# Where the last tile's norm stands at the end of two output products

## Chip, core and metric

The kernel runs on one core of a Trainium2 chip. The metric is the device time of one execution in microseconds (us); the median of several runs is given. TensorE (PE) does the matrix products, ScalarE (ACT) activations and casts, VectorE (DVE) sums of two tiles, GpSimd (POOL) here little beside the roots of the norms, SyncE (SP) issues most DMAs.

## The reference

Two layers over 1024 tokens of 1024 features. The first mixes by attention, the second by a recurrent block; both end with a dense SwiGLU block. Each sub-layer is normed before and behind:

```python
for layer in range(DEPTH):
    h = rmsnorm(x, norm_mix_pre[layer])
    m = attention_mixer(h, ...) if layer % 2 == 0 else recurrent_mixer(h, ...)
    x = x + rmsnorm(m, norm_mix_post[layer])
    h = rmsnorm(x, norm_ffn_pre[layer])
    x = x + rmsnorm(swiglu(h, ...), norm_ffn_post[layer])
```

Both mixers end with a product by an output matrix, `m = y @ w_out`. What matters here is the stretch from that product through the two norms to the first gate and up products of SwiGLU.

## The kernel before

**Precision and tiles.** Most products take each operand as a sum of two rounded parts (hi and lo) and make three passes: hi by hi, hi by lo, lo by hi. Tokens go in eight tiles of 128.

**The output product** (`out_product`, called once in each layer) runs over tiles 0 to 2, then 3 to 5, then 6 and 7, each time over eight blocks of the inner size. The last four blocks of tiles 6 and 7 are done in plain float32 (L662, matmuls at L585), so that their weights need no split; they sit in buffers of the tag "w".

**The norm of a tile** (`norm`, which calls `post_norm_of`, and `pre_norm`) has these steps:

- first squares on ACT (L178 through `rstd`), of the product in PSUM, summed along the row;
- the root of the mean on POOL (L182, L183);
- the gain of the post norm on DVE (L250), which reads the same PSUM tile as the squares and is run behind them;
- the residual on DVE (L256): rows times root plus x; it is stored by SP (L258);
- second squares on ACT (L178 again) of the new x, and their root on POOL (L182, L183);
- the scaling by that root on ACT (L212), called `scaled`;
- the turn: eight transposes on PE (L222) into two PSUM tiles;
- the take (`HiddenS.take`): ACT copies both out (L85), DVE forms four sums of blocks in the one buffer of the tag "tf", ACT casts to the hi parts (L96) and DVE subtracts for the lo parts (L89).

**The gate's operands.** SwiGLU's products are made by Strassen's scheme in seven products of blocks. `first` calls `gate_load`, which scales the gate's weights by the gain of the norm (L700) and forms their sums and differences on DVE (L719 to L726), with a cast (L712) and a subtraction (L713) for each of seven operands. Then it sets up the seven products over the first 256 columns, which come from tiles 0 to 3. `strassen` is a generator: the caller draws products from it, so that PE has work between the turns of the last tiles: one product, tile 6's turn, four products, tile 7's turn, two products. Next come the same seven products over the other 256 columns, which need tiles 4 to 7, and then the up product (`gate_up`), whose weights are scaled behind the last cast of tile 7's take.

**What sets the order.** A planner puts every engine's instructions in a fixed order: among those that it takes to be ready it picks by rank. `behind` adds edges to it: each instruction traced inside the block comes after the named ones that run on the same engine. It makes no wait between engines. Each engine then works through its list in that order. `last_m` holds the first squares (ACT) and the gain (DVE) of a tile; `first` returns `last`, the last cast (ACT) and the last subtraction (DVE) of the gate's operands.

Of the kernel before, what the change touches and what calls it, by code (L numbers as in the profile page):

```python
# [12 lines left out]
ALU = mybir.AluOpType  # L13
# [14 lines left out]
def rows(t, x):  # L28

    if not isinstance(t, tuple):  # L30
        return [(slice(0, P), x[t * P:(t + 1) * P, :])]
    r, a = t
    o = [2 * a * P + k * P + 64 * r for k in range(2)]
    return [(slice(64 * k, 64 * k + 64), x[o[k]:o[k] + 64, :]) for k in range(2)]
# [65 lines left out]
class Trunk:  # L100
# [134 lines left out]
    def post_norm_of(self, ms, mg, x_src, x_dst, t, gpost, sink, pool, x=None):  # L235

        nc = self.nc
        if x is None:  # L240
            x = pool.tile([P, D], F32, tag="nx", bufs=2, name=self.uid("x"))
        for d, s in rows(t, x_src):
            self.load(x[d, :], s)
        junk = pool.tile([P, D // len(ms)], BF16, tag="junk", bufs=1, name=self.uid("junk"))

        squares_first = mg is ms[0][1] or len(ms) == 1
        if squares_first:
            rs = self.rstd(pool, [m for _, m in ms], junk)
        for c, m in ms:
            scaled = nc.vector.tensor_tensor(mg[:, c], m, gpost[:, c], op=ALU.mult).ins  # L250
        if not squares_first:
            rs = self.rstd(pool, [m for _, m in ms], junk)
        self.last_m = [self.squared, scaled]

        def rest(later=False):
            nc.vector.scalar_tensor_tensor(x, mg, rs, x, op0=ALU.mult, op1=ALU.add)  # L256
            for k, (d, s) in enumerate(rows(t, x_dst)):
                (nc.scalar if k and sink is None else nc.sync).dma_start(s, x[d, :])  # L258
            if sink is not None:
                return self.pre_norm(pool, x, mg, None, sink, t, self.psum_t, later)  # L260

        return rest
# [299 lines left out]
    def out_product(self, ap, pp, first, aT, w, x_src, x_dst, gpost_v, sink, kts):  # L562

        nc = self.nc
# [16 lines left out]
        def matmuls(ps, passes, first, last):  # L581

            for n in range(2):
                for i, (x, y) in enumerate(passes):
                    self.matmul = nc.tensor.matmul(ps[:, n * 512:(n + 1) * 512], x, y[:, n, :], start=first and i == 0,  # L585
                                     stop=last and i == len(passes) - 1).ins

        def norm(t, ps):
            mg = ap.tile([P, D], F32, tag="mg", bufs=3, name=self.uid("mg"))

            x = self.apool.tile([P, 1152], F32, tag="first", name=self.uid("x"))[:, :D] if t in (2, 5) else None
            return self.post_norm_of([(slice(0, D), ps)], mg, x_src, x_dst, t, gpost, sink, ap, x)
# [6 lines left out]
        for t0 in (0, 3):  # L599
# [30 lines left out]
            last_m = self.last_m  # L630
# [27 lines left out]
        for t in range(2):  # L658
            for i in range(4):

                with self.behind([self.matmul] + ([self.turned[3 + i]] if t == 0 and i < 3 else [])):
                    matmuls(pst[t], [(acts[i][:, t * P:(t + 1) * P], rows[i])], False, i == 3)  # L662
            if t == 0:
                rest = norm(6, pst[0])
                last_m = self.last_m
                turn6 = rest(True)
                scaled = self.scaled


        last, products, hold = first(last_m, psum)  # L670
        with self.behind([scaled, *last]):
            rest = norm(7, pst[1])
        last_m = self.last_m
        turn7 = rest(True)
# [577 lines left out]
```

## Time and profile before

| | |
|---|---|
| median of 3 runs | 2198.3 us (2197.07 to 2202.79) |
| the profiled execution, its own time | 2198.43 us |
| its span | 2196.6 us |
| PE busy | 2161.5 us (98%) |
| DVE busy | 1540.9 us (70%) |
| ACT busy | 1171.1 us (53%) |
| POOL busy | 217.7 us (10%) |
| granted TensorE clock, mean | 0.997 |

Busy time says how long an engine had an instruction in hand. The span is the time from the first to the last instruction; the time of an execution holds 1.8 us more. A timeline lists instructions of an engine by their start, and in brackets how long it had stood idle and whose result ended that. The granted clock is the share of full speed that PE was given. PE is nearly always busy, so what can be won without less work lies in the few places where it waits or runs at a lower clock.

### The profile page before, as it was taken

The numbers are of one execution on the slowest core, as the hardware profiler recorded it, in microseconds if no ns is written. First come the engines' busy times: TensorE is split into PE (matmuls) and PEld (weight loads), VectorE is DVE, ScalarE is ACT, GpSimd is POOL, SyncE is SP. The second block draws the span as 40 slices with busy tenths as digits, with TensorE's granted clock in tenths as the row PEclk, the third lists the DMA queues.
The fourth block names the chain that finished last, engine by engine and source line by source line (L and its number), as shares of the span: only waits on it lengthen the run. The fifth ranks groups of instructions, "written<-read, shape, count | busy, mean of one in ns | idle before, by whom it ended". The sixth has DMA issues, their size and how long they took to land.

```text
span 2196.6 us, 30590 instructions
## 1 busy us (share of the span) xinstructions
PE 2161.5 (98%) x11140; PEld 1803.2 (82%) x11140; DVE 1540.9 (70%) x2526; ACT 1171.1 (53%) x2174; POOL 217.7 (10%) x450
## 2 busy tenths in 40 slices
PE   9999999999999999999999999999999999999998
PEld 8888889878788888888887777888788888888886
DVE  5877865656878777776767677437787777758675
ACT  6655555556755444443446676528754444424443
POOL 2111113121100000000001333102000000000011
PEclk9999999999999999999999999999999999999999
DMA  7101011126323333336468411356233333328565
GB/s 273 34 30 49 27 37 49 54 84 221 137 91 111 117 98 115 94 123 230 144 183 253 130 58 39 100 192 221 86 120 106 101 112 99 115 87 287 172 182 155
DMA packets 168279, 270.21 MB, mean 123 GB/s; under 512 B 13889, under 2 KB 94785, under 8 KB 168129
## 3 DMA queue, kind: packets, MB, share of 16 engines
q1 hardware_dynamic: 167488, 266.18, 37.8%
q10 hardware_dynamic: 640, 2.10, 0.3%
q8 instruction: 87, 1.43, 0.3%
q14 instruction: 64, 0.52, 0.1%
HBM read 202.69 MB, written 65.54 MB: 122 GB/s over the span
## 4 chain that ended last, share of the span: by engine, by line
PE 87%; DVE 5%; DMA 3%; ACT 3%; issue 2%; POOL 0%; SPq 0%; POOLq 0%; ACTq 0%; DVEq 0%
PE ps L742 12%; PE ps L744 12%; PE ps L743 12%; PE ps L585 8%; PE ps L827 5%; PE ps L829 5%; PE ps L828 5%; PE tr L427 3%; PE pso L356 3%; PE psq L166 2%; PE psq L167 2%; PE psq L168 2%; PE ps L166 2%; PE ps L167 2%; PE ps L168 2%
## 5 line engine op out<-in xcount | busy, mean ns | idle before, releaser
L742 PE MATMUL ps<-hS,q 128*128 128x512 f32 (+1 forms) x1288 | 490.2, 381 | 0.7 <-ACT hS L96 0.4
L743 PE MATMUL ps<-hS,q 128*128 128x512 f32 (+1 forms) x1288 | 489.6, 380 | 0.9 <-DVE hS L89 0.9
L744 PE MATMUL ps<-hS,q 128*128 128x512 f32 (+1 forms) x1288 | 489.0, 380 | 0.0
L713 DVE TENSOR_TENSOR q<-raw,q 128x512 fp32r<-128x512 f32 x308 | 204.5, 685 | 181.6 <-ACT q L712 181.0
L743 PEld LDWEIGHTS ps<-hS,q 128*128 128x128 f32 x1288 | 242.7, 188 | 47.7 <-DVE hS L89 1.3
L742 PEld LDWEIGHTS ps<-hS,q 128*128 128x128 f32 x1288 | 242.3, 188 | 47.3 <-ACT hS L96 0.8
L744 PEld LDWEIGHTS ps<-hS,q 128*128 128x128 f32 x1288 | 242.7, 188 | 45.9
L712 ACT CAST q<-raw 128x512 fp32r<-128x512 f32 x308 | 177.7, 616 | 162.5 <-DVE raw L721 129.4
L828 PE MATMUL ps<-o,o 128*128 128x512 f32 x616 | 240.0, 390 | 0.5 <-DVE o L823 0.5
L829 PE MATMUL ps<-o,o 128*128 128x512 f32 x616 | 238.0, 390 | 0.5 <-DVE o L957 0.5
L700 ACT ACTIVATE raw<-raw,gcol 128x256 f32<-128x256 f32 x352 | 150.3, 498 | 143.3 <-DMA raw<-in_ffn_w_up_dram 71.6
L827 PE MATMUL ps<-o,o 128*128 128x512 f32 x616 | 221.4, 391 | 3.3 <-ACT o L956 3.0
L822 ACT CAST o<-raw 128x512 fp32r<-128x512 f32 x184 | 110.8, 621 | 160.3 <-PE ps L829 59.1
L182 POOL TENSOR_SCALAR rs<-ss 128x1 f32<-128x1 f32 x52 | 24.6, 473 | 1423.6 <-ACT junk L178 1356.9
L823 DVE TENSOR_TENSOR o<-raw,o 128x512 fp32r<-128x512 f32 x184 | 123.1, 686 | 56.1 <-ACT o L822 55.3
L827 PEld LDWEIGHTS ps<-o,o 128*128 128x128 f32 x616 | 115.5, 188 | 30.2 <-ACT o L956 4.8
L828 PEld LDWEIGHTS ps<-o,o 128*128 128x128 f32 x616 | 115.6, 188 | 25.3 <-DVE o L823 1.5
L829 PEld LDWEIGHTS ps<-o,o 128*128 128x128 f32 x616 | 115.6, 188 | 25.1 <-DVE o L957 1.4
L156 DVE TENSOR_TENSOR wlo<-raw,whi 128x1024 fp32r<-128x1024 f32 x76 | 93.4, 1228 | 58.5 <-ACT whi L155 57.8
L411 DVE TENSOR_TENSOR_SCAN pr<-pr,zero 128x128 f32<-128x128 f32 (+7 forms) x64 | 86.8, 1360 | 30.7 <-POOL pr L408 25.7
L155 ACT CAST whi<-raw 128x1024 fp32r<-128x1024 f32 x76 | 79.7, 1050 | 50.2 <-PE ps L167 19.9
L166 PE MATMUL psq<-hT,whi 128*128 128x512 f32 x256 | 101.8, 397 | 0.1
(206 smaller groups left out, 4314.2 us busy)
## 6 DMA issues: line engine op xcount, KB each, us to landing
raw<-in_ffn_w_gate_dram SPq DMA_DIRECT2D x44, 512.0 KB, 4.2
raw<-in_ffn_w_up_dram SPq DMA_DIRECT2D x44, 512.0 KB, 4.2
gS<-c SPq DMA_DIRECT2D x88, 256.0 KB, 3.6
raw<-gS SPq DMA_DIRECT2D x88, 256.0 KB, 2.8
gA<-c SPq DMA_DIRECT2D x66, 256.0 KB, 3.4
raw<-in_ffn_w_down_dram SPq DMA_DIRECT2D x63, 256.0 KB, 4.4
raw<-gA SPq DMA_DIRECT2D x44, 256.0 KB, 2.8
t<-in_ffn_w_down_dram SPq DMA_DIRECT2D x22, 512.0 KB, 6.8
```

Of the source, the lines that this page charges most:

```text
L166: nc.tensor.matmul(ps, wh[:, kt, cols], hh[:, kt, :], start=kt == 0, stop=False)
L585: self.matmul = nc.tensor.matmul(ps[:, n * 512:(n + 1) * 512], x, y[:, n, :], start=first and i == 0, stop=last and i == len(passes) - 1).ins
L700: nc.scalar.activation(raw[:, i], raw[:, i], AF.Copy, scale=gain[:, 4 * k + i:4 * k + i + 1])
L712: self.last = nc.scalar.copy(t[:, 0], src).ins
L713: self.last_lo = nc.vector.tensor_tensor(t[:, 1], src, t[:, 0].bitcast(F32), op=ALU.subtract).ins
L742: nc.tensor.matmul(ps, a[:, 0, kt, :], bh, start=kt == 0, stop=False)
L743: nc.tensor.matmul(ps, a[:, 0, kt, :], bl, start=False, stop=False)
L744: self.matmul = nc.tensor.matmul(ps, a[:, 1, kt, :], bh, start=False, stop=kt == 3).ins
L823: tt(t[:, 1], src, t[:, 0].bitcast(F32), op=ALU.subtract)
L827: nc.tensor.matmul(ps, a[0], b[:, 0], start=first, stop=False)
L828: nc.tensor.matmul(ps, a[0], b[:, 1], start=False, stop=False)
L829: nc.tensor.matmul(ps, a[1], b[:, 0], start=False, stop=last)
```

## The change

```diff
         def rest(later=False):
-            nc.vector.scalar_tensor_tensor(x, mg, rs, x, op0=ALU.mult, op1=ALU.add)
+            self.summed = nc.vector.scalar_tensor_tensor(x, mg, rs, x, op0=ALU.mult, op1=ALU.add).ins
...
                 turn6 = rest(True)
-                scaled = self.scaled
+                squared, summed = self.squared, self.summed
...
-        last, products, hold = first(last_m, psum)
-        with self.behind([scaled, *last]):
+        last, products, hold = first([*last_m, summed], psum)
+        with self.behind([squared]):
             rest = norm(7, pst[1])
```

Two edges change, in both output products.

- The last operands of the gate (`S3`, `S1` and `S4`, and the sum at L726 from which `S4` is made) stood on DVE behind tile 6's gain. Now they stand behind tile 6's residual (`summed`) too. On ACT nothing changes for them: their casts stand behind tile 6's first squares.
- Tile 7's first squares stood on ACT behind tile 6's scaling and the last cast of the gate's operands, and its gain on DVE behind the last of their subtractions. Now the squares stand behind tile 6's second squares (`self.squared`, which `pre_norm` has set last), and the gain has no edge of its own.

No instruction is added or taken away. The edges of the turns, the takes and the products stay as they are.

## The prediction

> **What bounds the kernel now.** I read the chain of work that ended last first, to see which engine sets the time.
>
> ```profile
> PE 87%; DVE 5%; DMA 3%; ACT 3%; issue 2%; POOL 0%; SPq 0%; POOLq 0%; ACTq 0%; DVEq 0%
> ```
>
> TensorE (PE) carries 87% of it. What the change can win is therefore time in which PE waits at the two places that it touches: the ends of the two output products. The next view is PE's timeline at the first of them. The columns are start, duration, engine, line, operation and count; in brackets stands the idle time before the row and who ended it.
>
> ```profile
> 571.46 10.47 PE L585 MATMUL ps<-raw,act 128*128 128x512 f32 x24
> ...
> 583.08 0.28 PE L744 MATMUL ps<-hS,q 128*128 128x256 f32 x1
> 585.33 1.09 PE L222 MATMUL pst<-ident,mg 128*128 128x128 f32 x8 [1.98 <-ACT mg L212]
> ...
> 591.89 0.28 PE L744 MATMUL ps<-hS,q 128*128 128x256 f32 x1
> 592.98 1.09 PE L222 MATMUL pst<-ident,mg 128*128 128x128 f32 x8 [0.81 <-ACT mg L212]
> 593.83 0.36 PE L742 MATMUL ps<-hS,q 128*128 128x256 f32 x1
> ...
> 597.50 0.39 PE L743 MATMUL ps<-hS,q 128*128 128x256 f32 x1 [0.45 <-DVE hS L89]
> ...
> 600.72 0.74 PE L742 MATMUL ps<-hS,q 128*128 128x256 f32 x4 [0.19 <-ACT hS L96]
> ...
> 608.00 0.40 PE L742 MATMUL ps<-hS,q 128*128 128x512 f32 x1
> ```
>
> The 24 matmuls of L585 end at 581.93. Twelve of the first gate product follow (the last starts at 583.08). Then PE stands still for **1.98 us**, until tile 6's scaled rows (L212) arrive for its eight transposes (L222). Four more products run to 592.17; then 0.81 us for tile 7's transposes, 0.45 us and 0.19 us for tile 7's hidden operands (L89, L96). At 608.00 the up product starts without a wait. So 3.43 us of waiting, all of it behind the norms of tiles 6 and 7.
>
> The same timeline at the second product:
>
> ```profile
> 1553.87 1.56 PE L222 MATMUL pst<-ident,mg 128*128 128x128 f32 x8 [1.97 <-ACT mg L212]
> ...
> 1562.09 1.03 PE L222 MATMUL pst<-ident,mg 128*128 128x128 f32 x8
> ...
> 1566.56 0.39 PE L743 MATMUL ps<-hS,q 128*128 128x256 f32 x1 [0.44 <-DVE hS L89]
> ...
> 1569.77 0.74 PE L742 MATMUL ps<-hS,q 128*128 128x256 f32 x4 [0.18 <-ACT hS L96]
> ...
> 1577.53 0.47 PE L742 MATMUL ps<-hS,q 128*128 128x512 f32 x1 [0.30 <-ACT c L784]
> ```
>
> The waits are 1.97, 0, 0.44, 0.18 and 0.30 us. But from tile 6's transposes to tile 7's it takes 1562.09 - 1553.87 = 8.22 us, without a wait at the end of it, where the first product needs 592.17 - 585.33 = 6.84 us for the same instructions. The table by windows says why; after the busy times it gives the granted clock, the DMA share and GB/s.
>
> ```profile
> 585.30:587.00 1.70, 1.67 (x15) 1.67 (x16) 0.69 (x1) 1.70 (x4) 0.55 (x2) 1.00 0.62 213
> ...
> 1555.10:1557.70 2.60, 2.60 (x14) 2.60 (x13) 2.51 (x3) 2.57 (x5) 0.59 (x2) 0.50 0.03 10
> ```
>
> After the second product's pause the clock is 0.50, after the first one's it is 1.00. The half clock costs 8.22 - 6.84 = **1.38 us**.
>
> Now what tile 6's scaled rows wait for: the timelines of ScalarE (ACT), VectorE (DVE) and GpSimd (POOL) in the first product.
>
> ```profile
> 575.10 1.02 ACT L178 ACTIVATE junk<-ps 128x1024 bf16<-128x1024 f32 x1 [0.67 <-PE ps L585]
> ...
> 578.53 0.62 ACT L712 CAST q<-raw 128x512 fp32r<-128x512 f32 x1 [0.70 <-PE ps L585]
> 580.25 0.62 ACT L712 CAST q<-raw 128x512 fp32r<-128x512 f32 x1 [1.10 <-PE ps L585]
> 580.77 1.05 ACT L178 ACTIVATE mg<-x 128x1024 f32<-128x1024 f32 x1
> ...
> 584.13 1.15 ACT L212 ACTIVATE mg<-x,rs 128x1024 f32<-128x1024 f32 x1 [2.21 <-POOL rs L183]
> 585.18 1.00 ACT L178 ACTIVATE junk<-ps 128x1024 bf16<-128x1024 f32 x1
> ...
> 594.21 1.05 ACT L96 CAST hS<-tf 128x1024 fp32r<-128x1024 f32 x1
> ...
> 599.62 1.05 ACT L96 CAST hS<-tf 128x1024 fp32r<-128x1024 f32 x1 [2.91 <-DVE tf L89]
> 600.57 3.30 ACT L700 ACTIVATE raw<-raw,gcol 128x256 f32<-128x256 f32 x8
> ```
>
> ```profile
> 576.25 1.23 DVE L250 TENSOR_TENSOR mg<-ps,g 128x1024 f32<-128x1024 f32 x1
> 577.39 0.68 DVE L726 TENSOR_TENSOR raw<-raw,raw 128x512 f32<-128x512 f32 x1
> 577.99 1.22 DVE L89 TENSOR_TENSOR hS<-tf,hS 128x1024 fp32r<-128x1024 f32 x1
> 579.12 1.28 DVE L256 SCALAR_TENSOR_TENSOR x<-mg,rs,x 128x1024 f32<-128x1024 f32 x1
> ...
> 583.25 0.43 DVE L89 TENSOR_TENSOR tf<-tf,mg 128x256 f32<-128x256 f32 x1
> 586.31 1.23 DVE L250 TENSOR_TENSOR mg<-ps,g 128x1024 f32<-128x1024 f32 x1 [2.64 <-ACT junk L178]
> 587.62 1.29 DVE L256 SCALAR_TENSOR_TENSOR x<-mg,rs,x 128x1024 f32<-128x1024 f32 x1
> ```
>
> ```profile
> 576.30 0.22 POOL L182 TENSOR_SCALAR rs<-ss 128x1 f32<-128x1 f32 x1 [9.05 <-ACT junk L178]
> ...
> 582.00 1.29 POOL L182 TENSOR_SCALAR rs<-ss 128x1 f32<-128x1 f32 x1 [4.83 <-ACT mg L178]
> 583.38 0.72 POOL L183 TENSOR_TENSOR rs<-rs,neghalf 128x1 f32<-128x1 f32 x1
> ```
>
> Tile 6: first squares on ACT at 575.10, gain on DVE (L250) at 576.25, residual (L256) at 579.12, second squares at 580.77, the two POOL steps of the root from 582.00, scaling (L212) at 584.13. ACT stood idle for 2.21 us before that scaling; tile 7's first squares, whose product had been ready since 581.93, came only behind it, at 585.18. DVE was idle for 2.64 us waiting for those squares.
>
> **The change, part by part.**
>
> *The gate's sums behind the residual.* On DVE, L726 (577.39, 0.60 to the next start) stands ahead of tile 6's residual now and must stand behind it. The cast of tile 4's sums (L89 at 577.99, 1.13) is bound by nothing new. If it stays ahead, the residual starts 0.60 earlier, at 578.52; if it goes behind too, at 577.39, 1.73 earlier. I take the first: that sub comes ahead of the residual today, although the residual's root was out (POOL's step at 576.30 took 0.22 us and the next one 0.57), so the planner thinks the root later than it is.
>
> The last cast of the gate block (ACT, 580.25) needs what L726 makes. It was started ahead of the second squares, after 1.10 us in which it held ACT's queue for a buffer that PE read. Behind the change its data come 0.6 us after the residual, so the second squares are ready first and pass it. They start when the residual ends: 579.12 + 1.28 = 580.40 now, less 0.60, so 579.80 and with a hand-over 579.85, against 580.77: **0.92 us** earlier. The bounds are 0 (the cast stays ahead) and 1.6 (the residual first on DVE; the cast at 578.53 keeps ACT until 579.15).
>
> From second squares to scaling it takes 584.13 - 580.77 = 3.36 us; the scaling then starts at 583.21.
>
> *Tile 7's first squares behind tile 6's second squares.* Free at 581.93, they take 1.00 and about 0.2 us for the sum's read: 582.0 to 583.2. That is just ACT's idle time, so whether they stand ahead of or behind the scaling costs 0 here; were they ahead and 0.5 us late (the moved cast between them), the scaling would be 0.5 us later. Tile 6's transposes follow the scaling by 585.33 - 584.13 = 1.20 us: at 584.41. PE's wait falls from 1.98 to 1.06 us, **0.92 won**; what is late there is still the root of tile 6.
>
> *Tile 7's transposes.* From its first squares to its transposes it takes 592.98 - 585.18 = 7.80 us. From 582.0 this gives 589.8. PE gets there at 584.41 + 6.84 = 591.25. The 0.81 us go: **1.73 us** won up to here. Tile 7's gain and residual (1.23 and 1.29) fill DVE's idle 2.64 us; no work is added. If that cover were gone, tile 5's sums (their last at 583.25) would come up to 2.5 us later.
>
> *Tile 7's operands.* PE's work between tile 7's transposes and the rest of the gate is 593.83 - 592.98 and 24 matmuls of 0.12, so 3.7 us. ACT's chain there is longer because tile 6's sums are cast (594.21, 0.95) between tile 7's two copies. With tile 7 not waited for, tile 6's cast has 1.4 us more and gets ahead of them. Then 0.45 and 0.19 us go too: **2.4 us** in the first product; if the cast stays between them, 1.7. The up product follows by ACT's chain too (the cast at 599.62, then 3.30 us of L700), which starts from the same cast of tile 7 and so moves along.
>
> *Second product.* The same steps win 0.92 us at tile 6. With a wait of 1.05 in place of 1.97 us I expect no drop of the clock, so another 1.38; then 0.44, 0.18 and 0.30: **3.2 us**. Tile 7 is ready in time: its first squares start at 1553.72 now,
>
> ```profile
> 1553.72 1.00 ACT L178 ACTIVATE junk<-ps 128x1024 bf16<-128x1024 f32 x1
> ```
>
> and 3.2 us earlier after; 7.80 us on is 1558.3, PE comes at 1552.95 + 6.84 = 1559.8.
>
> The wait added (tile 7's first squares behind tile 6's second squares) holds nothing that was earlier before. No DMA is added; tile 7's store is issued by SP some 3 us earlier, the two gate loads beside it aren't needed before L700 at 600.57. Sum: 2.4 + 3.2 = **5.6 us**. What can be won at most are all of PE's waits there and the half clock: 3.43 in the first, 1.97 + 1.38 + 0.92 = 4.27 in the second, 7.7 us.
>
> **The rivals.**
>
> 1. *The half clock stays.* For my reading: both places where I found it away from the start follow a pause. The other one, in the attention:
>
> ```profile
> 452.00:454.00 2.00, 0.44 (x2) 0.30 (x2) 1.94 (x8) 1.64 (x5) 0.25 (x1) 1.00 1.02 401
> 456.00:458.00 2.00, 2.00 (x9) 1.70 (x9) 0.49 (x3) 1.98 (x9) 1.13 (x3) 0.50 0.42 156
> ```
>
> PE was busy for 0.44 of 2 us, and the clock fell to 0.50. Against it: the first product's pause of 1.98 us cost no clock, so length alone doesn't decide, and a pause of 1.06 us may still do it, or the shifted one in the first product may now. Price: 1.38 us each. One: 4.2 us won, 2194.2. Two: 2.8 us, 2195.6. In the Trainium skill, "TensorE: Matmul & The Clock Gate", Part 1, the clock falls after an idle window of some 3.4 us that runs free of the kernel. By that rule no pause here is long enough to halve the clock; this trace disagrees (1.97 us did), though it bears out that phase matters. Taken literally the episode would then not go away with the pause, which is this rival.
>
> 2. *The root is the bound.* POOL's first step took 0.22 us at 576.30 beside the gain, 1.29 at 582.00 beside DVE's sums. Its second step, over the kernel:
>
> ```profile
> L183 POOL TENSOR_TENSOR rs<-rs,neghalf x56: 567/568/1457, 518.0 to 2189.9; 128x1 f32<-128x1 f32 x56
> ```
>
> With 1.46 instead of 0.72 there, tile 6 wins 0.2 instead of 0.92 in each product: 5.6 - 1.4 = 4.2 us, 2194.2. With both short (0.22 and 0.57) the scaling starts 1.22 us earlier, at 581.99, and PE's wait at tile 6 goes but for 0.1 us. Tile 7's squares then follow the scaling at 583.1, though, and its transposes are ready at 583.1 + 7.80 = 590.9 against 591.25 in the forecast: 0.35 us more in each, 6.3 us, 2192.1. The Trainium skill, "SBUF — State Buffer", Who interferes with whom, has a DVE instruction with two SBUF inputs block a GpSimd instruction that reads SBUF. By it the moved sums, all of that kind, can fall on tile 6's root as they do now; that leaves the sum as it is.
>
> 3. *The change does nothing for tile 6*: the planner keeps the last cast ahead of the second squares. Then only the 0.81 us and the operands' waits go, 1.45 us in the first and 0.92 in the second: 2.4 us, 2196.0.
>
> 4. *Slower.* Tile 7's gain and residual now compete on DVE. If they are put ahead of tile 5's sums, the chain of sums is pushed by up to 1.23 + 1.29 = 2.5 us; it has one buffer, so tile 5's push passes to tiles 6 and 7, whose cast (599.62) sets the rest of the gate and the up product. This decides from the point where it exceeds the 2.4 us won: with tile 6's transposes not earlier, 2.5 us lost in each, 2203.4; with a second half clock in each product beside it, 2206.2. Against it: tile 5's sums end at 583.25 + 0.43, and tile 7's gain can't start before 583.2.
>
> **How the numbers follow.** The profiled execution took 2198.43 us (span 2196.6 us), the median of the runs is 2198.3 us: the sum holds for both within 0.1 us. 2198.4 - 5.6 = 2192.8 us. Chances: the forecast with its bounds (4.5 us to the 7.7 us there are) 0.51; one or two half clocks 0.15; the root longer 0.06, shorter 0.07; nothing for tile 6: 0.12; slower 0.09. Range: 2190.4 to 2197.8; it reaches from the 7.7 us and a little for the scatter of the runs (2197.07 to 2202.79) to all but the last case and a part of the one before. A measurement of this kernel can tell about 0.3%, 6.6 us, from no change. The forecast lies inside it; only the upper end of the first case and of the shorter root lies beyond: 0.17 faster. Of the slower case the part with half clocks, 0.04, is beyond on the other side, which leaves 0.79 within.
>
> **What would show it.** Right: tile 7's first squares on ACT between tile 6's second squares and its scaling, or straight behind that scaling at an earlier time; L726 behind the residual; PE's wait ahead of tile 6's transposes near 1.0 us, none ahead of tile 7's; a granted clock of 1.00 in all windows of the second product. Wrong: the last gate cast still ahead of tile 6's second squares; a clock of 0.50 behind a pause of 1 us; tile 5's sums behind tile 7's residual; or a stage far from the two products that the planner orders anew and that loses what was won.

## The result and the profile after

| | median, us | runs | ratio to before (95%) |
|---|---|---|---|
| before | 2198.64 (2196.07 to 2202.79) | 6 | |
| changed | 2191.82 (2189.53 to 2193.45) | 6 | 0.997 (0.9959 to 0.998) |

The medians differ by 6.8 us; 5.6 us were forecast, a time of 2192.8 us. The difference is 0.31% of the time, so it stands just at the 0.3% at which this kernel can be told from no change, and the interval reaches to both sides of it. The time lies in the range that was given, 1.0 us below the forecast. The profiled execution took 2193.34 us (span 2191.5 us).

PE's timeline at the first output product of the changed kernel:

```profile
570.37 10.47 PE L585 MATMUL ps<-raw,act 128*128 128x512 f32 x24
...
583.13 1.09 PE L222 MATMUL pst<-ident,mg 128*128 128x128 f32 x8 [0.87 <-ACT mg L212]
...
589.82 1.04 PE L222 MATMUL pst<-ident,mg 128*128 128x128 f32 x8
...
593.56 0.28 PE L742 MATMUL ps<-hS,q 128*128 128x256 f32 x1
594.07 0.39 PE L743 MATMUL ps<-hS,q 128*128 128x256 f32 x1 [0.23 <-DVE hS L89]
594.29 0.28 PE L744 MATMUL ps<-hS,q 128*128 128x256 f32 x1
...
596.92 0.64 PE L742 MATMUL ps<-hS,q 128*128 128x256 f32 x4
...
604.12 0.40 PE L742 MATMUL ps<-hS,q 128*128 128x512 f32 x1
```

And at the second:

```profile
1539.02 10.47 PE L585 MATMUL ps<-raw,act 128*128 128x512 f32 x24
...
1551.82 1.09 PE L222 MATMUL pst<-ident,mg 128*128 128x128 f32 x8 [0.92 <-ACT mg L212]
...
1558.50 1.04 PE L222 MATMUL pst<-ident,mg 128*128 128x128 f32 x8
...
1562.75 0.39 PE L743 MATMUL ps<-hS,q 128*128 128x256 f32 x1 [0.23 <-DVE hS L89]
...
1572.81 0.40 PE L742 MATMUL ps<-hS,q 128*128 128x512 f32 x1
```

The 24 matmuls of L585 are the same work in every kernel here, and so, but for one experiment that adds transposes, is all that PE does from their start to the first 128x512 matmul of the up product. I call the time between these two starts **the stretch** and measure each kernel by it. Before, it took 608.00 - 571.46 = 36.54 us in the first product and 37.53 us in the second (1577.53 less the 1540.00 at which the 24 matmuls started there). Now it takes 604.12 - 570.37 = **33.75** and 1572.81 - 1539.02 = **33.79 us**: 2.79 and 3.74 us less, 6.5 together.

PE's wait at tile 6 fell from 1.98 to 0.87 us, the one at tile 7 is gone, and of the two for operands one is left, of 0.23 us. PE's waits in the second product are nearly those of the first now. The clock behind its pause, from the table by windows (busy times, then granted clock, DMA share, GB/s):

```profile
1552.70:1555.30 2.60, 2.60 (x24) 2.60 (x23) 2.51 (x3) 2.23 (x5) 0.00 (x0) 1.00 0.73 219
```

The clock is 1.00, where it was 0.50. ACT, DVE and POOL in the first product of the changed kernel:

```profile
578.73 1.06 ACT L178 ACTIVATE mg<-x 128x1024 f32<-128x1024 f32 x1 [0.68 <-DVE x L256]
...
579.79 0.60 ACT L712 CAST q<-raw 128x512 fp32r<-128x512 f32 x1
580.93 1.02 ACT L178 ACTIVATE junk<-ps 128x1024 bf16<-128x1024 f32 x1 [0.54 <-PE ps L585]
...
581.94 1.14 ACT L212 ACTIVATE mg<-x,rs 128x1024 f32<-128x1024 f32 x1
...
589.20 1.05 ACT L96 CAST hS<-tf 128x1024 fp32r<-128x1024 f32 x1 [0.50 <-DVE tf L89]
590.51 1.07 ACT L85 COPY mg<-pst 128x512 f32<-128x512 f32 x2 [0.26 <-PE pst L222]
...
595.38 1.05 ACT L96 CAST hS<-tf 128x1024 fp32r<-128x1024 f32 x1 [2.84 <-DVE tf L89]
```

```profile
577.42 1.28 DVE L256 SCALAR_TENSOR_TENSOR x<-mg,rs,x 128x1024 f32<-128x1024 f32 x1
578.62 0.68 DVE L726 TENSOR_TENSOR raw<-raw,raw 128x512 f32<-128x512 f32 x1
...
582.03 0.41 DVE L89 TENSOR_TENSOR tf<-tf,mg 128x256 f32<-128x256 f32 x1
582.37 1.21 DVE L250 TENSOR_TENSOR mg<-ps,g 128x1024 f32<-128x1024 f32 x1
```

```profile
579.97 0.35 POOL L182 TENSOR_SCALAR rs<-ss 128x1 f32<-128x1 f32 x1 [3.89 <-ACT mg L178]
580.40 0.60 POOL L183 TENSOR_TENSOR rs<-rs,neghalf 128x1 f32<-128x1 f32 x1
```

L726 (578.62) stands behind tile 6's residual (577.42), and the last gate cast (579.79) behind the second squares (578.73), both as forecast. Tile 7's first squares (580.93) stand ahead of tile 6's scaling (581.94), and that scaling starts with no idle time of ACT in front of it. POOL had the root out at 580.40 + 0.60 = 581.00. So it is ACT's own order, not the root, that holds the scaling now.

In the second product of this execution DVE ran later against PE. Tile 6's second squares:

```profile
1548.06 1.06 ACT L178 ACTIVATE mg<-x 128x1024 f32<-128x1024 f32 x1 [1.35 <-DVE x L256]
```

They start 1548.06 - 1539.02 = 9.04 us behind the 24 matmuls, against 8.36 in the first product and 9.31 in both products before. PE's wait is no longer for that (0.92 us against 0.87), since the scaling is held by tile 7's first squares here too. The same lateness is seen in the first product of one of the repeats below, and in neither product of the other.

### The profile page after: what moved, and what is told of

Same layout as the page of the kernel before. It is cut to its first block, busy times and chain, and to the rows that moved or that the text cites. A ratio compares the mean times of both kernels' runs of the same rounds, so it can differ in the third digit from the quotient of the medians.

```text
span 2191.5 us, 30594 instructions
## 1 busy us (share of the span) xinstructions
PE 2159.3 (99%) x11140; PEld 1801.2 (82%) x11140; DVE 1542.0 (70%) x2526; ACT 1171.0 (53%) x2174; POOL 224.8 (10%) x450
## 4 chain that ended last, share of the span: by engine, by line
PE 87%; DVE 5%; DMA 3%; issue 2%; ACT 2%; POOL 0%; SPq 0%; POOLq 0%; ACTq 0%; DVEq 0%
PE ps L743 13%; PE ps L742 13%; PE ps L744 13%; PE ps L585 7%; PE ps L827 5%; PE ps L829 5%; PE ps L828 5%; PE tr L427 3%; PE pso L356 3%; PE psq L166 2%; PE psq L167 2%; PE psq L168 2%; PE ps L167 2%; PE ps L166 2%; PE ps L168 2%
## 5 line engine op out<-in xcount | busy, mean ns | idle before, releaser
L742 PE MATMUL ps<-hS,q 128*128 128x512 f32 (+1 forms) x1288 | 489.6, 381 | 0.0
L742 PEld LDWEIGHTS ps<-hS,q 128*128 128x128 f32 x1288 | 241.8, 188 | 46.3 <-DVE tf L89 0.2
```

The lines of the kernel that those rows point to most:

```text
L742: nc.tensor.matmul(ps, a[:, 0, kt, :], bh, start=kt == 0, stop=False)
```

## The experiments

The times of each are against runs of the kernel before on the same chip; the stretches are those of its profiled execution.

### The sums behind the residual, alone

```diff
-                squared, summed = self.squared, self.summed
+                scaled, summed = self.scaled, self.summed
...
-        with self.behind([squared]):
+        with self.behind([scaled, *last]):
```

This is against the changed kernel: tile 7's first squares stand where they stood before.

> The gate's sums stand behind tile 6's residual as in the changed kernel, tile 7's norm stands where it stood before. Measure: from the start of the 24 last matmuls of L585 to the first matmul of the up product (before: 36.54 us in the first output product, 37.53 in the second; changed kernel: 33.75 and 33.79). Theory (the moved sums carry the win; tile 7's squares ahead of the scaling cost tile 6 as much as they win for tile 7): tile 6's scaling starts as soon as its root is out, PE's wait ahead of tile 6's transposes falls under 0.3 us, tile 7's squares follow the scaling, PE waits 0.7 to 1.0 us ahead of tile 7's transposes; 33.9 to 34.4 us in both products, no half clock in the second. Rival (each edge wins its own part): PE's wait at tile 6 falls to 0.9 us and the one at tile 7 stays at 0.8: 35.2 to 35.6 us in the first.

Measured: 2193.08 us (11 runs) against 2197.82 (27), ratio 0.9978 (0.9969 to 0.9987). Stretches 34.56 and 35.02 us. Three views of its first product, ACT, POOL and PE:

```profile
579.85 1.06 ACT L178 ACTIVATE mg<-x 128x1024 f32<-128x1024 f32 x1 [0.68 <-DVE x L256]
...
582.15 1.16 ACT L212 ACTIVATE mg<-x,rs 128x1024 f32<-128x1024 f32 x1 [0.64 <-POOL rs L183]
583.21 1.00 ACT L178 ACTIVATE junk<-ps 128x1024 bf16<-128x1024 f32 x1
```

```profile
581.09 0.35 POOL L182 TENSOR_SCALAR rs<-ss 128x1 f32<-128x1 f32 x1 [3.89 <-ACT mg L178]
581.52 0.59 POOL L183 TENSOR_TENSOR rs<-rs,neghalf 128x1 f32<-128x1 f32 x1
```

```profile
583.36 1.09 PE L222 MATMUL pst<-ident,mg 128*128 128x128 f32 x8
...
591.01 1.09 PE L222 MATMUL pst<-ident,mg 128*128 128x128 f32 x8 [0.81 <-ACT mg L212]
```

The profile shows no wait at tile 6 any more: the transposes come 11.88 us behind the start of the 24 matmuls (583.36 - 571.48), against 13.87 before. They start 0.26 us behind the last matmul (583.10), where the unhindered ones of the changed kernel start 0.12 us behind it (589.82 and 589.70), so they still wait for the scaling by about 0.14 us. POOL's first step took 0.35 us in place of 1.29, so the root took 581.52 + 0.59 - 579.85 = 2.26 us from the start of the squares. The scaling starts 582.15 - 571.48 = 10.67 us behind the 24 matmuls; in the changed kernel it is 581.94 - 570.37 = 11.57. The **0.90 us** between them is the price of tile 7's squares standing ahead of the scaling. But with them behind it, tile 7 waits as it did before: 0.81 us, and 591.01 - 583.21 = 7.80 us from its first squares to its transposes, the very chain that the prediction had measured. The waits came as expected, but both stretches are longer than the 33.9 to 34.4 us expected: the operands' waits stay as they were before (0.44 and 0.20 us in the first product, 0.44, 0.18 and 0.32 in the second).

### Tile 7's first squares moved, alone

```diff
-        last, products, hold = first([*last_m, summed], psum)
+        last, products, hold = first(last_m, psum)
```

> Tile 7's norm stands as in the changed kernel, the gate's sums stand where they stood before. Theory: tile 6's second squares stay behind the last gate cast, so PE's wait at tile 6 stays at 1.98 us; tile 7's squares fill ACT's wait for the root, PE's wait at tile 7 goes, and some 0.4 us later: 35.2 to 35.5 us in the first product; in the second the pause of 1.97 us and the half clock stay: 36.6 to 37.0. Rival (tile 7's squares carry most of the win): 34.3 us or less in the first.

Measured: 2193.07 us (11 runs) against 2197.82, ratio 0.998 (0.9971 to 0.9989). Stretches 34.73 and 34.72 us. POOL, PE and the table by windows in its second product:

```profile
1548.28 1.29 POOL L182 TENSOR_SCALAR rs<-ss 128x1 f32<-128x1 f32 x1 [4.83 <-ACT mg L178]
```

```profile
1551.45 1.09 PE L222 MATMUL pst<-ident,mg 128*128 128x128 f32 x8 [1.82 <-ACT mg L212]
...
1558.14 1.03 PE L222 MATMUL pst<-ident,mg 128*128 128x128 f32 x8
```

```profile
1551.45:1554.00 2.55, 2.55 (x22) 2.55 (x23) 1.52 (x2) 2.01 (x4) 0.00 (x0) 1.00 0.61 215
```

POOL's first step took 1.29 us again, and tile 6 is waited for as long as before (1.82 us). Tile 7 is not: its squares (at 1548.30) now fill ACT's idle time in front of the scaling (1550.25), and its transposes start at 1558.14 without a wait. The pause of 1.82 us cost no clock. Both stretches are shorter than expected (35.2 to 35.5 and 36.6 to 37.0 us): the second had been expected with a half clock, and in the first the waits in brackets fell by 1.38 us in all but the stretch by 1.82, a difference that comes back in the account of the prediction.

Against the undisturbed stretches of the kernel before, 36.55 and 37.01 us (the next experiment), the first edge alone wins 1.99 and 1.99 us, the second alone 1.82 and 2.29, and both 2.80 and 3.22. The two are not a sum: with one alone 8.1 us would add up, together it is 6.0. The first edge removes the wait at tile 6, the second gives 0.87 us of it back and removes the wait at tile 7.

### The half clock: the pause filled, and the same kernels again

The first of these, against the kernel before, puts 14 more transposes in front of tile 6's turn, into a tile that the turn's own then overwrite. PE has work in the pause; nothing that follows is earlier.

```diff
-                ps = psum()
+                ps = psum(); [nc.tensor.transpose(ps[:, 0:P], self.ident, self.ident) for _ in range(14) if (t, q) == (6, 0)]
```

> The kernel before with 14 more transposes of the identity (about 1.5 us of PE's time) into the bank that tile 6's transposes then overwrite, behind the first gate product and ahead of tile 6's transposes: nothing else waits for them. They take up PE's pause at tile 6 and leave tile 6 and tile 7 where they are. Theory (the pause makes the half clock, and tile 7's chain of 7.8 us from its squares hides a part of it): clock 1.00 in the second product, which falls from 37.53 to about 37.0, with a wait of about 0.8 us at tile 7 as in the first; the first stays at 36.5. Rival A (the half clock costs 1.38 us by itself): 36.1 in the second. Rival B (the half clock comes whatever the pause): 0.50 and 37.5 in the second.

Measured: 2198.01 us (11 runs) against 2197.82, ratio 1.0 (0.9991 to 1.0009). Stretches 36.56 and 37.01 us. PE in its second product:

```profile
1540.75 10.47 PE L585 MATMUL ps<-raw,act 128*128 128x512 f32 x24
...
1554.62 1.09 PE L222 MATMUL pst<-ident,mg 128*128 128x128 f32 x8 [0.44 <-ACT mg L212]
...
1562.27 1.09 PE L222 MATMUL pst<-ident,mg 128*128 128x128 f32 x8 [0.81 <-ACT mg L212]
...
1577.76 0.47 PE L742 MATMUL ps<-hS,q 128*128 128x512 f32 x1 [0.30 <-ACT c L784]
```

The pause is down to 0.44 us, the clock is whole, and still only 37.53 - 37.01 = **0.52 us** are won in the second product, not 1.38. At full clock PE is at tile 7's turn early and waits 0.81 us for it, as in the first product: the transposes start 1562.27 - 1540.75 = 21.52 us behind the 24 matmuls. At half clock they started 1562.09 - 1540.00 = 22.09 us behind them, without a wait. Only the 0.57 us between these was lost to the half clock up to there. The 37.0 us are as expected; that the pause makes the half clock, as the expectation had it, the next two runs don't bear out.

The kernel before, unchanged, twice more:

> The kernel before, unchanged, for one more profile. Theory (whether a pause of some 2 us halves the clock hangs on when it falls, not on the product): of the pauses in this and the next profile some have a clock of 1.00 and some 0.50 behind them; where it is 1.00 in the second product, the way from the start of the last 24 matmuls of L585 to the first matmul of the up product is 37.0 us as with the pause filled. Rival (the second product always gets the half clock): 0.50 and 37.5 us in the second product, 1.00 and 36.5 in the first, in both profiles.

> The kernel before once more: as in the run ahead of this one.

They took 2198.37 and 2198.59 us, one run each. The first, PE in its second product and the window behind the pause:

```profile
1540.92 10.46 PE L585 MATMUL ps<-raw,act 128*128 128x512 f32 x24
...
1554.78 1.09 PE L222 MATMUL pst<-ident,mg 128*128 128x128 f32 x8 [1.98 <-ACT mg L212]
...
1562.43 1.09 PE L222 MATMUL pst<-ident,mg 128*128 128x128 f32 x8 [0.80 <-ACT mg L212]
...
1577.93 0.47 PE L742 MATMUL ps<-hS,q 128*128 128x512 f32 x1 [0.32 <-ACT c L784]
```

```profile
1554.80:1557.40 2.60, 2.60 (x23) 2.60 (x24) 1.55 (x2) 2.60 (x6) 0.79 (x2) 1.00 0.41 139
```

The same pause, 1.98 us, and no half clock: the stretch takes 1577.93 - 1540.92 = 37.01 us, as in the experiment before. The other repeat shows 37.02, and both 36.55 or 36.56 in the first product. Of six pauses of 1.97 or 1.98 us in three profiles of this kernel, one had the half clock behind it. It came in one execution of three, then, and these runs don't show that the change ended it. Nor did these two profiles bring the mixture of half and whole clocks that was expected of them.

The changed kernel, unchanged, twice more, each beside other experiments:

> The changed kernel, unchanged, on the same chip as the kernels beside it. Theory: 33.7 to 33.9 us in both products and a clock of 1.00, a median of 2190.5 to 2192.5 us. Rival (the changed kernel's pause of 0.9 us halves the clock too, now and then): 34.3 us or more in one of them with a clock of 0.50.

> The changed kernel on the same chip, to hold against the run ahead of this one: 33.7 to 33.9 us in both output products, a median of 2190 to 2192 us.

2190.51 us (9 runs) against 2197.71 (19), ratio 0.997 (0.996 to 0.998); 2192.13 (5) against 2199.33 (15), ratio 0.9963 (0.995 to 0.9977). Stretches 33.76 and 33.75, 33.79 and 33.76 us. The stretches are as expected, and the difference of 7 us repeats. The stretches account for 36.55 + 37.01 - 33.77 - 33.77 = 6.0 us of it. The last 1 us I can't place: from the up product of the first layer to the second output product, code that the change doesn't touch, the profiled execution took 1539.02 - 604.12 = 934.9 us and the first repeat 930.9 us, so single executions of one kernel differ there by 4 us.

### Filling what is left at tile 6

0.87 and 0.92 us of waiting remain at tile 6. The next three give PE more work in front of tile 6's turn, against the changed kernel. The first moves the point at which the generator hands PE over behind its second product:

```diff
-        yield self.matmul
         p2 = product("A12", 1)
+        yield self.matmul
```

> The changed kernel with two gate products instead of one ahead of tile 6's transposes (three instead of four between the two turns). Theory (PE's last wait at tile 6 is only a lack of work there; tile 7 is ready in time): the 1.44 us product covers the 0.9 us wait, tile 7's transposes come 0.9 us earlier and at most 0.2 us of wait there: 32.8 to 33.1 us in both products, 1.5 to 1.8 us less in all than the changed kernel. Rival (tile 7's norm is the bound): the wait comes back ahead of tile 7's transposes or at tile 7's operands, 33.6 us or more.

Measured: 2191.05 us (5 runs) against 2197.82, ratio 0.9968 (0.9956 to 0.9981). Stretches 33.84 and 33.84 us. PE and ACT in its first product:

```profile
583.55 0.39 PE L742 MATMUL ps<-hS,q 128*128 128x256 f32 x1 [1.14 <-ACT first L748]
```

```profile
582.10 1.14 ACT L212 ACTIVATE mg<-x,rs 128x1024 f32<-128x1024 f32 x1
583.14 0.36 ACT L748 COPY first<-ps 128x256 f32<-128x256 f32 x1
```

The wait hasn't gone, it has moved ahead of the second product (L742) and grown to 1.14 us: that product goes into the other half of the first one's PSUM tile, and the copy that empties the first half (L748) stands on ACT behind the same scaling. In place of the scaling, its successor is waited for. The stretch is 0.1 us longer than the changed kernel's, and not at the 32.8 to 33.1 us expected.

The second takes the product with S2 forward instead, into another PSUM tile:

```diff
-        yield self.matmul
+        ps2 = product("S2", 4); yield self.matmul
         p2 = product("A12", 1)
-        tt(u2, product("S2", 4), s1, op=ALU.add)
+        tt(u2, ps2, s1, op=ALU.add)
...
-                    ps = new_psum()
-                    halves.extend([ps[:, 512:768], ps[:, 0:256]])
+                    ps, pt = new_psum(), new_psum()
+                    halves.extend([pt[:, 512:768], ps[:, 512:768], pt[:, 0:256], ps[:, 0:256]])
```

> The changed kernel with the product of S2 moved ahead of tile 6's transposes and into another PSUM tile than the first product, so that it does not wait for ACT's copy of that one. Theory (PE's wait of 0.9 us at tile 6 is only a lack of work, and with two products ahead it was the copy that stood behind the scaling): no wait ahead of tile 6's transposes nor of S2, 32.8 to 33.2 us in both products, 1.2 to 2 us faster than the changed kernel. Rival (the win is taken back at tile 7's transposes or at DVE's sum that frees S2's bank): 33.6 us or more.

Measured: 2197.09 us (11 runs) against 2197.71, ratio 1.0001 (0.9992 to 1.001). Stretches 37.26 and 35.91 us: by the time, all that the change won is lost, as the expectation's rival had it. PE in its first product, and a window:

```profile
584.51 1.04 PE L222 MATMUL pst<-ident,mg 128*128 128x128 f32 x8
...
590.78 1.09 PE L222 MATMUL pst<-ident,mg 128*128 128x128 f32 x8 [0.93 <-ACT mg L212]
...
595.31 0.39 PE L743 MATMUL ps<-hS,q 128*128 128x256 f32 x1 [0.44 <-DVE hS L89]
...
598.51 0.80 PE L742 MATMUL ps<-hS,q 128*128 128x256 f32 x2 [1.64 <-ACT hS L96]
```

```profile
598.00:600.00 2.00, 1.49 (x7) 1.49 (x8) 1.23 (x1) 2.00 (x6) 0.00 (x0) 0.55 0.00 0
```

There is no wait at tile 6, but 0.93 us at tile 7, 0.44 and 1.64 at the operands, and a half clock behind these. On DVE the sum of a product (L751, 584.77) now stands ahead of tile 7's residual (585.11), and on ACT tile 6's copies and casts (L85 at 585.20, L96 at 586.31) ahead of tile 7's second squares (587.14); these squares start 15.81 us behind the 24 matmuls, against 14.76 in the changed kernel. The second product has the same waits without a half clock; it is 37.26 - 35.91 = 1.35 us shorter. Without a half clock this order would thus still be ahead of the kernel before (36.55 and 37.01 us); how often it comes, one profile doesn't tell.

The third is the first of this group with all products in PSUM tiles dealt out so that the second doesn't share a tile with the first:

```diff
-                if not halves:
-                    ps = new_psum()
-                    halves.extend([ps[:, 512:768], ps[:, 0:256]])
-                return halves.pop()
+                i, h = plan.pop(0)
+                if i == len(tiles):
+                    tiles.append(new_psum())
+                return tiles[i][:, 512 * h:512 * h + 256]
```

with `plan = [(0, 0), (1, 0), (0, 1), (2, 0), (1, 1), (2, 1), (3, 0)]` set ahead of it, and the move of the generator's hand-over as above.

> As the kernel with two gate products ahead of tile 6's transposes, and the first two products in different PSUM tiles (the seven are spread over four tiles in another order), so that the second doesn't wait for ACT's copy of the first. Theory (that wait of 1.14 us was the copy, which stands behind the scaling on ACT): no wait at the second product nor at either turn, 32.6 to 33.0 us from the start of the last 24 matmuls of L585 to the first matmul of the up product in both output products, 1.5 to 2.3 us faster than the changed kernel. Rival (tile 7's chain ends last): the wait turns up ahead of tile 7's transposes or operands or of the up product, 33.5 us or more.

Measured: 2193.9 us (11 runs) against 2199.33, ratio 0.9974 (0.9966 to 0.9983). Stretches 34.06 and 34.02 us. PE in its first product, and at the up product of its second:

```profile
586.45 1.03 PE L222 MATMUL pst<-ident,mg 128*128 128x128 f32 x8
...
591.07 0.39 PE L742 MATMUL ps<-hS,q 128*128 128x256 f32 x1 [0.71 <-DVE first L752]
...
597.15 0.39 PE L743 MATMUL ps<-hS,q 128*128 128x256 f32 x1 [0.50 <-DVE hS L89]
```

```profile
1574.96 0.47 PE L742 MATMUL ps<-hS,q 128*128 128x512 f32 x1 [0.57 <-DVE c L751]
```

Again no wait at tile 6 (586.45), and again it comes back: 0.71 us for a sum on DVE (L752) that empties a PSUM tile, 0.50 for tile 7's operands; in the second product it is 0.52 us at the operands and 0.57 at the up product. The rival was right here too.

In none of the three could tile 6's wait be filled without another coming up: two waits of 0.87 and 0.23 us in the changed kernel's first product, 1.14 us in the first of the three, 0.71 and 0.50 in the third. There is also less to be had than 0.87 us: tile 7's last cast ends at 595.38 + 1.05 = 596.43 us in the changed kernel, and the product that had waited for it before (L742, four in a row) starts at 596.92, so tile 7's chain would be next after 0.5 us. None of these kernels is measurably faster than the changed one.

## Why the prediction was nearly right

**The residual** (0.60 earlier): right in the first product. From the 24 matmuls' start it comes at 577.42 - 570.37 = 7.05 us, before at 579.12 - 571.46 = 7.66.

**The second squares** (0.92 earlier): right in the first product; 8.36 us in place of 9.31, and the last gate cast was passed as described. In the second product of the profiled execution neither step holds: the residual came no earlier than before (1546.75 - 1539.02 = 7.73 us), and the squares 0.27 us earlier (9.04). The scaling came 1.05 us earlier all the same (1550.63 - 1539.02 = 11.61 us, before 1552.66 - 1540.00 = 12.66). There it was the shorter root that did it, which the next step had left out.

**"From second squares to scaling it takes 3.36 us"**: failed as a step. I carried the root's 1.29 and 0.72 us over from before; it took 0.35 and 0.60. The step of 1.29 us belongs to the order on DVE: it appears at tile 6's second root in the kernel before and in the experiment that leaves the sums where they were, and 0.35 in the one that moves only the sums. That was the short root of rival 2.

**"Whether they stand ahead of or behind the scaling costs 0"**: failed too. It held only because the root was taken as late; with the root out at 581.00 the squares ahead of it cost 0.90 us. The two errors nearly cancel: the scaling moved by 12.67 - 11.57 = 1.10 us where 0.92 was forecast, and PE's wait is 0.87 and not 1.06. Rival 2 had the squares behind the scaling in this case; the planner put them ahead.

**Tile 7's transposes**: right. Their wait is gone in both products, and the 7.80 us were met to the hundredth where the chain was left as it was.

**The operands' waits go**: mostly right. Tile 6's cast (589.20) got ahead of tile 7's copies (590.51), the 0.19 us went, and 0.23 of the 0.45 us stayed.

**The first product's 2.4 us**: mis-sized. The waits that went sum to 3.43 - 0.87 - 0.23 = 2.33 us, but the stretch fell by 2.79. The other 0.46 us the brackets don't hold. They count from the modelled end of the last matmul, 0.28 us behind its start, although the next one starts 0.12 us behind it when PE is kept busy. In the first view of the changed kernel, from 593.56 to 594.29 it takes 0.73 us for two steps that take 0.24: a loss of 0.49 us at a bracket of 0.23. Four waits became two, so the term was short by about 0.23 us for each wait that went. With tile 7's squares moved alone, two waits went as well, and the brackets were short by about as much (1.82 - 1.38 = 0.44 us).

**"No drop of the clock, so another 1.38"**: the clock was whole, but the term was wrong. What the half clock had cost is 0.52 us, since it covered the 0.81 us at tile 7; and the two other profiles of the kernel before didn't have it at all. Against the undisturbed 37.01 us the second product won 3.2 us, the size that was forecast, but made up of the wait at tile 7, 0.80 us that the prediction had taken as absent there, of those at the operands and at the up product, and of what the brackets leave out. That the sum of 5.6 us came so near to the 6.0 us of the undisturbed stretches is therefore in part luck: a half clock priced too high stood in for waits priced too low.

**The rivals.** The half clock didn't stay (1), and tile 6 did gain (3). Slower (4): tile 5's sums ended at 582.03 + 0.41 us, just as tile 7's gain started at 582.37, so nothing was pushed.

## What to carry to other kernels

Where an engine with a fixed order waits at two places for two chains, an edit's worth at one place depends on the other chain: the edges here win 2.0 us and 1.8 to 2.3 us alone and 2.8 to 3.2 us together in each product. An edge that lets an instruction pass another should be priced with the other's data early as well as late; a cost of 0 that rests on a stall elsewhere is a cost as soon as that stall goes. A disturbance seen once in a profile, such as a half clock, should be looked for in a second profile of the same kernel before its price enters a sum.

## What the runs showed of the chip

**The half clock doesn't follow from the length of a pause alone.** One of six equal pauses of 1.97 or 1.98 us was followed by it, neither of the two of 1.82 us, and in the kernel with S2 taken forward one of two equal runs of waits (0.93, 0.44 and 1.64 us within 8 us). It cost 1.35 us (37.26 - 35.91) where PE was the bound and 0.52 us (37.53 - 37.01) where a chain beside it hid the rest. The Trainium skill, "TensorE: Matmul & The Clock Gate", Part 1, has a window of some 3.4 us that runs free of the kernel: the spread over equal pauses agrees with that, but an idle time of that length was not needed here, where 1.97 us was followed by the half clock once.

**A GpSimd step on 128 numbers took between 0.22 and 1.29 us in these stretches, and moving DVE's instructions beside it changed its time.** It took 0.22 us beside the gain, which reads PSUM and SBUF (576.30 before), 0.35 us beside the sums as they now stand, and 1.29 us beside them as they stood before. In the second product of the changed kernel, where DVE ran later and was at its sums instead of the gain, the step of tile 6's first root took 0.72 us (1543.86). The Trainium skill, "SBUF — State Buffer", Who interferes with whom, has a DVE instruction with two SBUF inputs hold up a GpSimd instruction that reads SBUF; the short and the long times agree with it, but why the same kind of sums costs 0.35 in one order and 1.29 in the other was not tried.
